# State-space constants moved to an earlier place and through DRAM, one rotation table for all batches, and gate weights loaded two jobs earlier, in a one-core decoder block

## The chip, the core and the metric

The kernel runs on one core of a Trainium2 chip. That core has five engines with an instruction stream each: TensorE (PE, the matrix multiplier, with its weight loads counted apart as PEld), VectorE (DVE), ScalarE (ACT), GpSimd (POOL) and SyncE (SP, which here issues nearly all DMAs). Each engine runs its stream in order and waits on semaphores for the others. The metric is the device time of one execution in microseconds (us), median over runs.

## What is computed

One decoder block over 16 meta tokens and 1024 positions of width 1024, in float32:

```python
h = layer_norm(concat(meta_tokens, x))
p = h @ w_in + b_in                     # columns: u_s5 | q | k | v | o | i | f | g_s5 | g_m
z = gelu(s5(u_s5)) @ s5_w_glu           # 32 groups of a complex diagonal recurrence
y_s5 = z[..., :D] * sigmoid(z[..., D:])
qk = silu(causal_conv(concat(q, k)))
hm = head_norm(mlstm(q, k, v, i, f))    # 4 heads, chunkwise
y_m = (sigmoid(o) * hm) @ m_w_out
mix = sigmoid(g_s5) * y_s5 + sigmoid(g_m) * y_m
h = layer_norm(alpha * h + mix @ w_o)
h = layer_norm(alpha * h + square(relu(h @ w_up + b_up)) @ w_down)
```

The S5 recurrence per group is x_t = Abar x_{t-1} + Bbar u_t with a complex diagonal Abar, and y_t = Re(C x_t) + D u_t. The kernel computes it in blocks of 8 positions: 130 blocks in a row, with matrices built from powers of Abar for what happens within a block, and a rotation table (the powers of Abar to the 8th, for 130 blocks) that turns the complex recurrence over blocks into a real scan.

## The kernel before

Float32 products are made of three passes: every operand is split into a high part (rounded to the matmul's format) and a low part (the rest), and `mm3` issues high x high, high x low and low x high (L226, L227, L228). A weight tile comes by DMA as `wraw`; ACT copies it to `whi` (L212) and DVE subtracts to get `wlo` (L213). This split is raised in priority, so that it stands early.

The program is a list of jobs. `ORDER` (L41) gives the first part: q0, q1, v0 and so on, where a q job makes q or k of one head (then the convolution), v the values and gates, o the output gate, u the S5 inputs, g an output gate's S5 half, m the matrices of the mLSTM output. Behind them come z0 to z7 (the GLU of the S5 output), then a stage `Seven` that computes the remaining gates and the mLSTM output product with seven products in place of eight (its left sides are sums and differences of blocks of h, its weights come pre-summed), then w_o and the feed-forward part.

Beside the jobs run *lanes*: generators that emit a few instructions at a time. `mm3` calls `pump(dt)` after every second term, which advances each lane by the time that the matmuls are reckoned to take; the numbers a lane yields (`C5`, `K5` and others, L44 to L55) are its pace. The lanes are ml (the mLSTM steps of the four heads), cv (convolution), s5c (S5 constants), s5 (S5 batches), s5g (GELU) and ah. A job `o` forces its head's mLSTM to be finished: it steps the lane until the head is ready. A scheduler then orders each engine's stream by its own reckoning of times; the order on each engine is fixed when the program is built.

Of an mLSTM step the document names: pk (L458), kw on ACT (L460), pS (L463), sw on DVE (L465), pn = C q (L473) and + v sw (L474), pu (L477), C updated on DVE (L482), the normaliser dd (L492 to L495), hraw on ACT (L496), the statistics (L497, L498). After four chunks come the head norm (ACT square root L172 with a table load, DVE L173 to L176, L506), eight transposes on PE (L513) and two copies on ACT (L514).

The S5 constants are made once for all (`s5_pre`, L579, started at job u0 by `S5_START`, L42) and then for each of four batches of eight groups when that batch's u tile is done (`s5_consts`, L674, added in L548): matrices `Mi` (input to state), `RS` (state to output), `Mx` (within a block) and the rotation table `T`, built by doubling: eight rounds of a complex product, six DVE operations each (L761 to L778). They stay in SBUF under `S5["m", b]`. `s5_batch` (L790) waits for them, then computes s5z on PE (L802), copies it by ACT and DVE (L812, L810), rotates it with T (L817 to L823), scans (L828), rotates back (L838 to L841), corrects (L846) and multiplies out on PE (L857, L858).

At z7 the pool `mid` is closed and a pool `ring` opened in its place; `begin()` loads eight blocks `rawb` of h (L991). After the last job, `first()` loads three tiles of gate weights into the ring (L1024), splits the first (L1042, L1043) and forms the differences of the h blocks (L1002), which become the left sides hT_hi (L997) and hT_lo (L998).

Of the kernel before, what the change touches and what calls it, by code (L numbers as in the profile page):

```python
# [9 lines left out]
F32 = mybir.dt.float32  # L10
# [4 lines left out]
P = 128  # L15
# [10 lines left out]
NB = LEN // 8  # L26
# [12 lines left out]
LN2_2 = math.log(2.0) - LN2_1  # L39
MAGIC = 1.5 * 2 ** 23  # L40
ORDER = "q0 q1 v0 q2 v1 q3 o1 o0 v2 o2 o3 u0 u1 v3 u2 g0 u3 g1 o4 o5 o7 o6 g2 g3 g5 g6 g4 g7 m0 m1"  # L41
S5_START = "u0"  # L42
NM = 2
SPLIT_UP = 200  # L44
PRE = 3
ZD = 1
ML = [2.4, 1.2, 1.68, 4.8]
NL = [0.88, 1.75, 1.75, 1.75]
C5 = [0.7, 0.98, 1.96, 0.49]
K5 = [1.7, 3.4, 1.7, 1.7]  # L50
Z5 = [1.0, 1.0, 1.0, 1.0]
D5 = [2.88, 1.22, 1.44, 1.44]
W5 = [2.21, 1.56, 2.6, 2.6]
# [59 lines left out]
def decoder_block(  # L113
# [80 lines left out]
    def load_w(job):  # L194
        job.raw = []
        for src, n in job.loads:
            r = slot("wraw") if ring[0] is None else ring[0].tile([P, 1024], F32, tag="wr", bufs=3, name="wraw")
            nc.sync.dma_start(r[:, :n], src)
            job.raw.append(r)

# [334 lines left out]
    def u_job(i):  # L535
        st = {}

        def evac(bi, c0, c1, ps):
            if bi == 0:
                st["u"] = slot("uT")  # L540
            o = st["u"][:, :LEN].rearrange("p (j c) -> p c j", j=8)
            a_.activation(o[:, c0 // 8:c1 // 8, :], ps.rearrange("p (c j) -> p c j", j=8), AF.Identity,
                          bias=bft[:, JU + i:JU + i + 1])

        def done():
            nc.sync.dma_start(us_dr[i * P:(i + 1) * P].rearrange("p j c -> p (j c)"), st["u"][:, :LEN])
            UD.add(i)
            lanes["s5c"].add(s5_consts(i))  # L548
            lanes["s5"].add(s5_batch(i))
        fm_job(JU + i, BLK, 0, evac, done)  # L550

# [118 lines left out]
        yield 1.3  # L670

    GEL = {}

    def s5_consts(b):  # L674
        E, ER = S5["E"], S5["ER"]
# [85 lines left out]
        T = slot("s5T")  # L761
        tc_, ts_ = (T[:, i * 520:(i + 1) * 520].rearrange("p (q c) -> p q c", q=4) for i in range(2))
        tmp = slot("s5tt")
        g_.memset(tc_[:, :, 0], 1.0)
        g_.memset(ts_[:, :, 0], 0.0)
        g_.tensor_copy(tc_[:, :, 1], S5["p8"][:, 0, q0:q0 + 4])
        g_.tensor_copy(ts_[:, :, 1], S5["p8"][:, 1, q0:q0 + 4])
        yield C5[b]
        n = 1
        while n < 129:  # L770
            m = min(n, 129 - n)
            sh = [P, 4, m]
            w1 = tmp[:, 0:4 * m].rearrange("p (q c) -> p q c", q=4)
            w2 = tmp[:, 512:512 + 4 * m].rearrange("p (q c) -> p q c", q=4)
            cmul(v_, tc_[:, :, n + 1:n + 1 + m], ts_[:, :, n + 1:n + 1 + m], tc_[:, :, 1:m + 1], ts_[:, :, 1:m + 1],
                 tc_[:, :, n:n + 1].to_broadcast(sh), ts_[:, :, n:n + 1].to_broadcast(sh), w1, w2)
            n *= 2
            yield C5[b]  # L778
        S5["m", b] = (RS, Mi, Mx, T)

    def u_load(b):
        U = slot("s5U")
# [221 lines left out]
    class Seven:  # L1004
# [8 lines left out]
        def load(self, i):  # L1013
            if i >= self.ntile():
                return
            r = ring[0].tile([P, 1024], F32, tag="wr", bufs=3, name="wraw")
            for j, (n, p) in enumerate(self.units[2 * i:2 * i + 2]):
                s = {5: 0, 6: 1, 7: 2, 3: 3}.get(n)
                if s is None:
                    t = self.w[self.i0 + 2 * p + (n == 4)].rearrange("p k f -> p (k f)")  # L1020
                    a = t[:, 0:512] if n == 1 else t[:, 512:1024]
                else:
                    a = ws_dr[self.p0 + p, s]
                tc.keep_in_program_order(nc.sync.dma_start(r[:, j * 512:j * 512 + 512], a))  # L1024
            self.raw[i] = r
# [117 lines left out]
    def gates_and_output():  # L1143
# [6 lines left out]
            for nm, kh, ch in (("12", 0, 1), ("22", 1, 1), ("11", 0, 0), ("21", 1, 0)):  # L1150
                R[nm] = raw_block(h_dr, kh, ch, META)

        def first():
            for i in range(3):
                g.load(i)
            g.split(0)
            sub(R["22"], R["12"], R["22"])
            sub(R["12"], R["12"], R["11"])
            sub(R["11"], R["11"], R["22"])
            to_home(R["11"], h01)  # L1160
            sub(R["21"], R["21"], R["11"])
            R.pop("11")
# [27 lines left out]
        return begin, first, run  # L1190

    def ln0_load(t):
        c0, n = rows0(t)
# [271 lines left out]
    jobs = all_jobs  # L1465
    ws = w_sums()
    next(ws)
    begin, first, run7 = gates_and_output()

    for i, j in enumerate(jobs):  # L1470
        if j.raw is None and j.w is None:
# [606 lines left out]
```

## Time and profile before

| what | before |
|---|---|
| median of 3 runs | 1565.78 us (1565.15 to 1569.24) |
| the profiled execution | 1566.04 us |
| its span in the trace | 1564.2 us |
| mean granted TensorE clock | 0.984 |
| DMA over the span | 261.32 MB, 137509 packets |

The span is what the profiler saw from the first to the last instruction; the rest of the profiled execution's time lies around it. The profile lists for each engine its busy time, a strip of 40 equal slices (39.1 us each) with tenths of busy time and of granted clock, groups of instructions by source line, and what ended the idle time before them. In the rows below, "out<-in" are the program's names for tiles.

### The profile page before, as it was taken

The numbers are of one execution on the slowest core, as the hardware profiler recorded it, in microseconds if no ns is written. First come the engines' busy times: TensorE is split into PE (matmuls) and PEld (weight loads), VectorE is DVE, ScalarE is ACT, GpSimd is POOL, SyncE is SP. The second block draws the span as 40 slices with busy tenths as digits, with TensorE's granted clock in tenths as the row PEclk, the third lists the DMA queues.
The fourth block names the chain that finished last, engine by engine and source line by source line (L and its number), as shares of the span: only waits on it lengthen the run. The fifth ranks groups of instructions, "written<-read, shape, count | busy, mean of one in ns | idle before, by whom it ended". The sixth has DMA issues, their size and how long they took to land.

```text
span 1564.2 us, 20543 instructions
## 1 busy us (share of the span) xinstructions
PE 1515.8 (97%) x7593; PEld 1278.7 (82%) x7593; DVE 1079.9 (69%) x2083; ACT 642.7 (41%) x982; POOL 102.2 (7%) x195
## 2 busy tenths in 40 slices
PE   8999999998999998989999999999999999999997
PEld 8998988996878886768788887888888888888886
DVE  7667555659867845677789675666666679766786
ACT  6523353333355433325534324444444534433340
POOL 0000001124031200000000001000000000000000
PEclk9999999998999999989999999999999999999999
DMA  8412324414354556775353328644443798667642
GB/s 311 159 57 61 100 62 129 122 37 112 104 129 103 164 182 218 279 269 195 108 170 114 108 76 247 225 158 149 147 149 123 248 363 322 230 229 236 216 166 108
DMA packets 137509, 261.32 MB, mean 167 GB/s; under 512 B 30768, under 2 KB 52984, under 8 KB 137352
## 3 DMA queue, kind: packets, MB, share of 16 engines
q1 hardware_dynamic: 111344, 233.00, 43.7%
q0 software_dynamic: 26064, 27.01, 7.1%
q8 instruction: 60, 0.98, 0.3%
q14 instruction: 41, 0.34, 0.1%
HBM read 188.78 MB, written 84.55 MB: 175 GB/s over the span
## 4 chain that ended last, share of the span: by engine, by line
PE 31%; issue 23%; DMA 3%; DVE 2%; ACT 0%; SPq 0%; POOL 0%; POOLq 0%; DVEq 0%
PE mm L228 7%; PE mm L227 7%; PE mm L226 7%; PE sd L227 3%; PE sd L226 3%; PE sd L228 3%; DMA wpre<-wu_dr 1%; DMA rawb<-h_dr 1%; DMA wu_dr<-wpre 1%; DMA wur<-in_wup_dram 0%; DVE wlo L1043 0%; DVE wlo L213 0%; DMA woraw<-in_wo_dram 0%; POOL wpre L1621 0%; SPq L991 0%
## 5 line engine op out<-in xcount | busy, mean ns | idle before, releaser
L226 PE MATMUL mm<-hT_hi,whi 128*128 128x512 f32 (+3 forms) x604 | 231.0, 382 | 8.0 <-ACT whi L1042 5.4
L228 PE MATMUL mm<-hT_hi,wlo 128*128 128x512 f32 (+3 forms) x604 | 226.7, 380 | 5.7 <-DVE wlo L213 3.7
L227 PE MATMUL mm<-hT_lo,whi 128*128 128x512 f32 (+3 forms) x604 | 229.1, 379 | 0.0
L226 PEld LDWEIGHTS mm<-hT_hi,whi 128*128 128x128 f32 x604 | 115.7, 192 | 26.6 <-ACT whi L1042 6.2
L228 PEld LDWEIGHTS mm<-hT_hi,wlo 128*128 128x128 f32 x604 | 115.0, 191 | 25.5 <-DVE wlo L213 4.3
L227 PEld LDWEIGHTS mm<-hT_lo,whi 128*128 128x128 f32 x604 | 115.6, 191 | 17.6 <-issue 0.4
L227 PE MATMUL sd<-dwl,dah 128*128 128x512 f32 x240 | 94.5, 394 | 0.0
L228 PE MATMUL sd<-dwh,dal 128*128 128x512 f32 x240 | 94.4, 394 | 0.0
L226 PE MATMUL sd<-dwh,dah 128*128 128x512 f32 x240 | 94.2, 393 | 0.0
L1773 ACT ACTIVATE dah<-da 128x1024 fp32r<-128x1024 f32 x56 | 58.7, 1052 | 86.2 <-PE sd L227 38.9
L1777 ACT ACTIVATE dwh<-wdr 128x1024 fp32r<-128x1024 f32 x56 | 58.9, 1053 | 84.0 <-DMA wdr<-in_wdn_dram 27.5
L1774 DVE TENSOR_TENSOR dal<-da,dah 128x1024 fp32r<-128x1024 f32 x56 | 68.2, 1219 | 23.8 <-ACT dah L1773 23.3
L228 PE MATMUL mm<-dwh,dal 128*128 128x512 f32 (+1 forms) x224 | 84.5, 378 | 0.0
L226 PE MATMUL mm<-dwh,dah 128*128 128x512 f32 (+1 forms) x224 | 84.4, 377 | 0.0
L227 PE MATMUL mm<-dwl,dah 128*128 128x512 f32 (+1 forms) x224 | 84.3, 377 | 0.0
L1778 DVE TENSOR_TENSOR dwl<-wdr,dwh 128x1024 fp32r<-128x1024 f32 x56 | 68.2, 1219 | 13.1 <-ACT dwh L1777 12.4
L226 PE MATMUL mm<-whi,hT_hi 128*128 128x256 f32 (+1 forms) x256 | 75.2, 294 | 0.0
L228 PE MATMUL mm<-whi,hT_lo 128*128 128x256 f32 (+1 forms) x256 | 74.7, 292 | 0.0
L227 PE MATMUL mm<-wlo,hT_hi 128*128 128x256 f32 (+1 forms) x256 | 73.8, 288 | 0.0
L213 DVE TENSOR_TENSOR wlo<-wraw,whi 128x1024 fp32r<-128x1024 f32 (+1 forms) x46 | 56.1, 1222 | 19.1 <-ACT whi L212 18.6
L228 PE MATMUL mm<-th,wul 128*128 128x512 f32 x156 | 61.6, 395 | 0.0
L227 PE MATMUL mm<-tl,wuh 128*128 128x512 f32 x156 | 61.5, 394 | 0.0
(474 smaller groups left out, 3703.1 us busy)
## 6 DMA issues: line engine op xcount, KB each, us to landing
da<-act_dr SPq DMA_DIRECT2D x56, 512.0 KB, 5.4
wdr<-in_wdn_dram SPq DMA_DIRECT2D x56, 512.0 KB, 6.3
wur<-in_wup_dram SPq DMA_DIRECT2D x32, 512.0 KB, 4.3
act_dr<-upy SPq DMA_DIRECT2D x64, 256.0 KB, 2.5
wraw<-in_wf_dram SPq DMA_DIRECT2D x30, 512.0 KB, 6.9
wu_dr<-wpre SPq DMA_DIRECT2D x21, 512.0 KB, 4.7
wpre<-wu_dr POOLq DMA_DIRECT2D x21, 512.0 KB, 5.0
act_dr<-upx SPq DMA_DIRECT2D x32, 256.0 KB, 2.8
```

The source lines that it names most:

```text
L213: todo.append(lambda e=v_, r=r, hi=hi, lo=lo, n=n: e.tensor_tensor(lo[:, :n], r[:, :n], f32(hi[:, :n]), op=OP.subtract))
L226: t_.matmul(ps, ah, bh, start=(i == 0 and part[0]), stop=False, skip_group_check=skip)
L227: t_.matmul(ps, ah, bl, start=False, stop=False, skip_group_check=skip)
L228: t_.matmul(ps, al, bh, start=False, stop=(i == n - 1 and part[1]), skip_group_check=skip)
L1773: a_.activation(ah[:, :D], a[:, :D], AF.Copy)
L1774: v_.tensor_tensor(alo[:, :D], a[:, :D], f32(ah[:, :D]), op=OP.subtract)
L1777: a_.activation(wh, raw[i], AF.Copy)
L1778: v_.tensor_tensor(wl, raw[i], f32(wh), op=OP.subtract)
```

## The change

`S5_START` becomes v0, the third job. There `s5_pre`, a new `s5_tables` and `s5_consts(0)` are queued in the lane s5c, and each `s5_consts(b)` queues the next. `s5_tables` builds one table for all 16 columns of constants in place of four (the products are four times as wide) and writes it to DRAM in four DMAs of 2048 pieces of 65 floats. `s5_consts` writes RS, Mi and Mx to DRAM, and `s5_batch` loads Mi, T, RS and Mx back. The pace numbers C5 and K5 of the lane change. The pool `mid` is closed and `ring` opened at z4 in place of z7, the first three tiles of gate weights are loaded at z6, ahead of the h blocks of z7, and the ring has four buffers in place of three.

```diff
-S5_START = "u0"
+S5_START = "v0"
...
-C5 = [0.7, 0.98, 1.96, 0.49]
-K5 = [1.7, 3.4, 1.7, 1.7]
+C5 = [1.9, 1.9, 1.9, 1.9]
+K5 = [1.7, 1.7, 1.7, 1.7]
...
-            r = slot("wraw") if ring[0] is None else ring[0].tile([P, 1024], F32, tag="wr", bufs=3, name="wraw")
+            r = slot("wraw")
...
             UD.add(i)
-            lanes["s5c"].add(s5_consts(i))
             lanes["s5"].add(s5_batch(i))
...
+    cs_dr = dram.tile([4, 3, P, 1024], F32, name="cs_dr")
+    ct_dr = dram.tile([2, P, 16, NB], F32, name="ct_dr")
+
+    def s5_tables():
+        lo, hi, tmp = ([slot("s5T"), slot("s5T")] for _ in range(3))
+        c1, s1 = (t[:, :1040].rearrange("p (q c) -> p q c", q=16) for t in lo)
+        c2, s2 = (t[:, :1040].rearrange("p (q c) -> p q c", q=16) for t in hi)
...
+        n = 1
+        while n < 64:
+            product(c1[:, :, n + 1:2 * n + 1], s1[:, :, n + 1:2 * n + 1], n, n, c1[:, :, 1:n + 1], s1[:, :, 1:n + 1],
+                    c1[:, :, n:n + 1], s1[:, :, n:n + 1])
+            n *= 2
+            yield 1.9
+        product(c2[:, :, 0:64], s2[:, :, 0:64], 64, 64, c1[:, :, 1:65], s1[:, :, 1:65], c1[:, :, 64:65], s1[:, :, 64:65])
+        yield 3.8
+        product(c2[:, :, 64:65], s2[:, :, 64:65], 128, 1, c1[:, :, 1:2], s1[:, :, 1:2], c2[:, :, 63:64], s2[:, :, 63:64])
+        for r in range(2):
+            nc.sync.dma_start(ct_dr[r, :, :, 0:65], (c1, s1)[r])
+            nc.sync.dma_start(ct_dr[r, :, :, 65:130], (c2, s2)[r])
...
-        S5["m", b] = (RS, Mi, Mx, T)
+        for i, t in enumerate((RS, Mi, Mx)):
+            nc.sync.dma_start(cs_dr[b, i], t[:, :1024])
+        CS.add(b)
+        if b < 3:
+            lanes["s5c"].add(s5_consts(b + 1))
...
-        while ("m", b) not in S5:
-            yield 0.5
-        RS, Mi, Mx, T = S5.pop(("m", b))
+        while b not in CS:
+            lanes["s5c"].step()
+        Mi, T, RS, Mx = (slot(n) for n in ("s5Mi", "s5T", "s5RS", "s5Mx"))
+        nc.sync.dma_start(Mi[:, :1024], cs_dr[b, 1])
...
-            r = ring[0].tile([P, 1024], F32, tag="wr", bufs=3, name="wraw")
+            r = ring[0].tile([P, 1024], F32, tag="wr", bufs=4, name="wraw")
...
-        def first():
+        def early():
             for i in range(3):
                 g.load(i)
+
+        def first():
             g.split(0)
...
         if j.tag == S5_START:
             lanes["s5c"].add(s5_pre())
+            lanes["s5c"].add(s5_tables())
+            lanes["s5c"].add(s5_consts(0))
...
-        if j.tag == "z7":
+        if j.tag == "z4":
             mid_ctx.close()
             ring_ctx = ExitStack()
             ring[0] = ring_ctx.enter_context(tc.tile_pool(name="ring", bufs=1, side="left"))
+        if j.tag == "z6":
+            early()
+        if j.tag == "z7":
             begin()
```

Line numbers in the rows of the change are its own: behind the new code they are 21 to 30 higher (L1024 becomes L1045, L991 becomes L1012, L817 becomes L838), while those of the mLSTM stay.

**PE, second half of head 0 and the start of v2.** Before, the head's last L474 (row 900) stands among matmuls of v2 (L226 to L228, `mm<-whi,hT_hi`), and its transposes follow 55 of them later, the last three of which are shown:

```order
953 L226 MATMUL mm<-whi,hT_hi 128x256
954 L227 MATMUL mm<-wlo,hT_hi 128x256
955 L228 MATMUL mm<-whi,hT_lo 128x256
956 L513 MATMUL pt<-ident,hraw 128x128 x2
957 L458 MATMUL pk<-ident,kT 16x128
958 L513 MATMUL pt<-ident,hraw 128x128 x2
959 L226 MATMUL mm<-whi,hT_hi 128x256
960 L513 MATMUL pt<-ident,hraw 128x128 x2
961 L227 MATMUL mm<-wlo,hT_hi 128x256
```

Now the step and the transposes follow each other, with S5 transposes (`s5p`) among them, ahead of v2's first matmuls (L340):

```order
909 L473 MATMUL pn<-C,qi 128x257
910 L474 MATMUL pn<-v_883,sw 128x257
911 L513 MATMUL pt<-ident,hraw 128x128 x2
912 L763 MATMUL s5p<-ident,s5P 128x128 x4
913 L513 MATMUL pt<-ident,hraw 128x128 x6
914 L763 MATMUL s5p<-ident,s5P 128x128 x4
915 L340 MATMUL mm<-whi,meta_hl 48x256 x8
```

The first half of the same head ends likewise; before, its two groups of four L513 stood among matmuls of o jobs. Now, ahead of the o0 job:

```order
849 L473 MATMUL pn<-C,qi 128x257
850 L474 MATMUL pn<-v_883,sw 128x257
851 L477 MATMUL pu<-v_883,kw 128x257
852 L513 MATMUL pt<-ident,hraw 128x128 x8
853 L458 MATMUL pk<-ident,kT 128x128
854 L463 MATMUL pS<-qT,kT 128x128
855 L473 MATMUL pn<-C,qi 128x257
856 L474 MATMUL pn<-v_883,sw 128x257
857 L477 MATMUL pu<-v_883,kw 128x257
858 L463 MATMUL pS<-qT,kT 128x128
859 L226 MATMUL mm<-hT_hi,whi 128x512
```

So the steps of the head have moved together, out of the matmuls of other jobs.

**DVE, end of the first half of head 3.** Before, the mLSTM rows (C, dd, sw, hst) stand here by themselves:

```order
794 L495 RECIPROCAL dd<-dd 128x1
795 L482 SCALAR_TENSOR_TENSOR C<-C,dec,pu 128x257
796 L497 BN_STATS hst<-hraw 128x6
797 L465 TENSOR_TENSOR sw<-pS,gB 128x128
798 L498 BN_AGGR hmv<-hst 128x2
```

Now S5 batch 3's rotation, scan and rotation back stand among them:

```order
719 L843 TENSOR_TENSOR s5Z<-s5w 128x520
720 L844 TENSOR_TENSOR s5Z<-s5w 128x520
721 L492 TENSOR_SCALAR dd<-pn 128x1
722 L849 SCALAR_TENSOR_TENSOR s5w<-s_r_993,s5Z 128x130 x4
723 L482 SCALAR_TENSOR_TENSOR C<-C,dec,pu 128x257
724 L849 SCALAR_TENSOR_TENSOR s5w<-s_r_993,s5Z 128x130
725 L493 SCALAR_TENSOR_TENSOR dd<-pn,ecol,dd 128x1
726 L849 SCALAR_TENSOR_TENSOR s5w<-s_r_993,s5Z 128x130 x3
727 L465 TENSOR_TENSOR sw<-pS,gB 128x128
728 L859 TENSOR_TENSOR s5Z<-s5w,s5T 128x512
729 L862 TENSOR_TENSOR s5w<-s5w,s5T 128x512
730 L495 RECIPROCAL dd<-dd 128x1
```

What moved is batch 3's work, which stood behind this half of the head before.

**SP, between the last z jobs and the gate stage.** Before (L1414 are the last writes of pre-summed feed-forward weights, L991 the h blocks, L1024 the gate weights):

```order
137 L198 DMA wraw<-in_wglu_dram 128x1024
138 L1414 DMA wu_dr<-wpre 128x1024 x7
139 L991 DMA rawb<-h_dr 128x2x512 x8
140 L1024 DMA wraw<-in_wf_dram 128x512 x6
141 L1024 DMA wraw<-ws_dr 128x512 x6
```

Now:

```order
167 L198 DMA wraw<-in_wglu_dram 128x1024
168 L1437 DMA wu_dr<-wpre 128x1024 x6
169 L1045 DMA wraw<-in_wf_dram 128x512 x6
170 L1437 DMA wu_dr<-wpre 128x1024
171 L1012 DMA rawb<-h_dr 128x2x512 x8
```

The six loads of gate weights changed places with the eight loads of h blocks, and stay behind six of the seven writes.

More of the change, by code (lines that the diff above doesn't have):

```diff
@@ L672, in decoder_block, with product @@
     GEL = {}
+    CS = set()
+    cs_dr = dram.tile([4, 3, P, 1024], F32, name="cs_dr")
[4 more added lines that the diff above has]
+        c2, s2 = (t[:, :1040].rearrange("p (q c) -> p q c", q=16) for t in hi)
+        g_.memset(c1[:, :, 0], 1.0)
+        g_.memset(s1[:, :, 0], 0.0)
+        g_.tensor_copy(c1[:, :, 1], S5["p8"][:, 0])
+        g_.tensor_copy(s1[:, :, 1], S5["p8"][:, 1])
+        yield 1.9
+        def product(oc, os, n, m, ac, as_, bc, bs):
+            w1, w2 = (t[:, 0:16 * m].rearrange("p (q c) -> p q c", q=16) for t in tmp)
+            sh = [P, 16, m]
+            cmul(v_, oc, os, ac, as_, bc.to_broadcast(sh), bs.to_broadcast(sh), w1, w2)
+        n = 1
[3 more added lines that the diff above has]
+            n *= 2
+            yield 1.9
+        product(c2[:, :, 0:64], s2[:, :, 0:64], 64, 64, c1[:, :, 1:65], s1[:, :, 1:65], c1[:, :, 64:65], s1[:, :, 64:65])
[4 more added lines that the diff above has]
+            nc.sync.dma_start(ct_dr[r, :, :, 65:130], (c2, s2)[r])
+        yield 1.9
     def s5_consts(b):
@@ L760, in s5_consts @@
         yield K5[b]
[L761 to L778, printed above, removed]
-        S5["m", b] = (RS, Mi, Mx, T)
+        for i, t in enumerate((RS, Mi, Mx)):
[3 more added lines that the diff above has]
+            lanes["s5c"].add(s5_consts(b + 1))
     def u_load(b):
@@ L793, in s5_batch @@
             yield 9.0
-        while ("m", b) not in S5:
-            yield 0.5
-        RS, Mi, Mx, T = S5.pop(("m", b))
+        while b not in CS:
+            lanes["s5c"].step()
+        Mi, T, RS, Mx = (slot(n) for n in ("s5Mi", "s5T", "s5RS", "s5Mx"))
+        nc.sync.dma_start(Mi[:, :1024], cs_dr[b, 1])
+        nc.sync.dma_start(T[:, :1040].rearrange("p (r q c) -> p r (q c)", r=2, q=4),
+                          ct_dr[:, :, 4 * b:4 * b + 4, :].rearrange("r p q c -> p r (q c)"))
+        nc.sync.dma_start(RS[:, :1024], cs_dr[b, 0])
+        nc.sync.dma_start(Mx[:, :1024], cs_dr[b, 2])
         uv = U[:, :8 * NB].rearrange("p (g c) -> p g c", g=8)
@@ L1189, in run @@
             y.run(lambda c, p: sdps() if c == "b" and p else mmps(), ym_evac, yhooks)
-        return begin, first, run
+        return early, begin, first, run
     def ln0_load(t):
@@ L1467, in decoder_block @@
     next(ws)
-    begin, first, run7 = gates_and_output()
+    early, begin, first, run7 = gates_and_output()
     for i, j in enumerate(jobs):
```

## The prediction, made before the changed kernel ran

> **What bounds the kernel now.** First the page's totals, then its clock line.
>
> ```profile
> PE 1515.8 (97%) x7593; PEld 1278.7 (82%) x7593; DVE 1079.9 (69%) x2083; ACT 642.7 (41%) x982; POOL 102.2 (7%) x195
> PEclk9999999998999999989999999999999999999999
> ```
>
> TensorE (PE) is busy for 97% of the span, so any change that keeps its matmuls, as this one does, can win only what PE waits, plus what it runs at a reduced clock. The two slices with an 8 are the 10th and the 18th: 352 to 391 us and 665 to 704 us. Next, what PE waited for. I asked the waits view stretch by stretch (waiting instruction, releaser, total, times, longest).
>
> ```profile
> PE gps L421 <- ACT gts L418: 2.0, 1, 2.0
> PE pu L477 <- ACT kw L460: 1.5, 1, 1.5
> ...
> PE mm L228 <- DVE wlo L213: 3.7, 1, 3.7
> PE s5k L741 <- DVE s5Ri L719: 2.9, 1, 2.9
> PE mm L226 <- DVE v L354: 1.3, 1, 1.3
> PE mm L226 <- ACT whi L212: 1.1, 1, 1.1
> ...
> PE mm L227 <- DVE gell L878: 3.1, 1, 3.1
> PE s5y L858 <- DVE s5w L846: 1.2, 1, 1.2
> ```
>
> The first two lie in 120 to 160 us, the next four in 340 to 400, the last two in 500 to 620. Then the same stretches as windows (busy time of each engine, granted clock, DMA share, GB/s):
>
> ```profile
> 160.00:340.00 180.00, 180.00 (x1139) 165.79 (x1138) 102.18 (x311) 72.22 (x118) 23.91 (x55) 1.00 0.33 92
> 365.00:390.00 25.00, 17.31 (x89) 14.49 (x89) 23.99 (x80) 10.37 (x15) 16.21 (x17) 0.73 0.41 113
> 455.00:480.00 25.00, 22.11 (x101) 17.24 (x101) 16.86 (x58) 16.76 (x22) 6.70 (x11) 1.00 0.28 60
> 670.00:680.00 10.00, 10.00 (x45) 8.13 (x44) 8.63 (x13) 3.82 (x6) 0.00 (x0) 1.00 0.97 366
> 690.00:700.00 10.00, 3.44 (x7) 2.32 (x8) 10.00 (x11) 3.17 (x3) 0.00 (x0) 0.57 0.58 202
> ```
>
> From 160 to 340 us PE never waits, with DVE at 57%. From 365 to 390 us DVE is full (23.99 of 25) and PE idles 7.7 us. Around 695 us PE waits again.
>
> **What the change removes.** (1) The table. Four doublings, one per batch, become one for all; the pile that fills DVE at 365 to 390 us goes. PE wins 3.7 + 2.9 + 1.3 + 1.1 = 9.0 us. The window's clock is 0.73, and at a floor of one half that means 0.27/0.5 x 25 = 13.5 us at half speed; 7.7 of the window are idle, and if 6 to 7 of the slow ones are busy, they lose half of themselves, about 3.5. Sum 12.5. (2) S5 ends earlier, before the GLU jobs: the waits for gell (3.1) and s5w (1.2) go, 4.3. (3) Waits at L421 and L477 (2.0 + 1.5) are taken over by a new pile there: 3.5. **Out: 20.3 us.**
>
> **What it adds.** The order of the changed kernel shows the same matmuls on PE, but other neighbours. I add up DVE's rows between two points at which it is tied to PE, and compare that with the matmuls that PE has there. Durations of one instruction (mean ns behind the bar):
>
> ```profile
> L817 DVE TENSOR_TENSOR s5w<-s5Z,s5T 128x520 f32<-128x520 f32 x4 | 2.8, 699 | 0.1
> L846 DVE TENSOR_TENSOR s5w<-s5Z,s5w 64x512 f32<-64x512 f32 x16 | 10.9, 684 | 0.2
> L828 DVE TENSOR_TENSOR_SCAN s5w<-s_r,s5Z 128x130 f32<-128x130 f32 x32 | 10.8, 401 | 0.0
> L213 DVE TENSOR_TENSOR wlo<-wraw,whi 128x1024 fp32r<-128x1024 f32 x40 | 48.8, 1222 | 19.1 <-ACT whi L212 18.6 <-DMA ys_dr<-s5Y 0.3
> L299 DVE SCALAR_TENSOR_TENSOR cy<-cpre,convt,cy 128x1040 f32<-128x1040 f32 x24 | 31.0, 1293 | 0.2
> L572 DVE TENSOR_TENSOR s5tt<-s5T 128x256 f32<-128x256 f32 x4 | 1.7, 425 | 0.1
> L514 ACT ACTIVATE hmF<-pt,mngt 128x512 f32<-128x512 f32 x16 | 10.5, 686 | 7.1 <-PE pt L513 7.1
> L460 ACT ACTIVATE kw<-pk,gB 128x128 f32<-128x128 f32 x28 | 10.1, 361 | 30.4 <-PE pk L458 30.3
> ```
>
> - **A, q2 to v1.** Six table products at each width: by the rows for 256 (0.43), 520 (0.70) and 1024 elements (1.22) the widths 1024, 512 and 256 cost 7.2, 4.0 and 2.4 us (overlap taken off), the narrower ones 3. With three convolution steps (1.29 each) and one of the like, five S5 products of 512 (0.65) and the wlo split itself, DVE has 25.3 us from v0's last eviction to the first wlo of v1; PE has 21.7 us of q2 by then (45 matmuls of 512 columns take 10 us). PE waits 3.6 us there, 0.8 to 2.9 more for the second wlo and conv rows between; I take 5.5. The gate rows behind them (L392, L405, L421) come 2.5 late. 8.0.
> - **B, first half of head 0.** One whole mLSTM step now stands between eight transposes L513 and the o0 job, without a matmul of another job. Ahead of the first L513, DVE has three L299 (3.9) and the head norm. Then k's activation on ACT and its multiply on DVE (some 3.5 with a table load, by rows of like size) stand ahead of the step's reciprocal, after which ACT runs L496, two L514, L460 and the whi split (0.47 + 0.69 + 0.69 + 0.36 + 1.05 = 3.3), and only then may o0's first matmul go. About 12 us against 5 of PE: 7.0.
> - **C, second half of head 0 and start of v2.** Here the trace shows the chain itself:
>
> ```profile
> 215.18 0.60 PE L474 MATMUL pn<-v,sw 128*128 128x257 f32 x2
> 215.81 0.16 DVE L492 TENSOR_SCALAR dd<-pn 128x1 f32<-128x1 f32 x1
> 216.51 0.47 ACT L496 ACTIVATE hraw<-pn,dd 128x256 f32<-128x256 f32 x1 [2.59 <-DVE dd L495]
> 217.00 1.28 ACT L172 ACT_TABLE_LOAD   x1
> 218.30 0.30 ACT L172 ACTIVATE hny<-hmv,eps_t 128x4 f32<-128x4 f32 x1
> 219.23 0.16 DVE L176 SCALAR_TENSOR_TENSOR hny<-hnu,hny 128x4 f32<-128x4 f32 x1
> 219.43 1.38 DVE L506 TENSOR_SCALAR hraw<-hraw,hmv,hny 128x256 f32<-128x256 f32 x4
> 222.11 0.38 PE L513 MATMUL pt<-ident,hraw 128*128 128x128 f32 x2
> ```
>
>   From the end of L474 to that of the first L506 (0.41) it is 4.1 us, and PE fills 6.3 to L513 with 55 matmuls of v2. In the changed order L513 stands right behind L474, so all 4.1 are bare; then two whi splits and a wlo (1.05, 1.05, 1.22) stand behind it on ACT and DVE before v2 can start, half hidden: 1.6. 5.7.
> - **Head 1**, where S5's copies now stand before L514, L460 and whi on ACT: 2.0.
> - **D, S5 batches 0 and 2** (their DVE work between mLSTM steps): 3.5.
> - **E, first half of head 3.** Batch 3's DVE work now falls among three mLSTM steps that PE issues with nothing between: six products of 520 (3.9 us, overlapped), eight scans (2.7), four of 512 (2.5), four L846 (2.7), and between them the steps' own rows and the head norm, about 5. That is 17 us to the L506 that L513 needs, while PE has 5: 12 to 13 us of wait. Before, the same place cost 2.9 (the 25 - 22.11 of 455 to 480 us). 10.
> - Clock after B, C and E: between 0 (455 to 480 us has 1.00 despite 2.9 us of waits) and 6 (half speed for 4 us after each, as at 690 to 700 with 0.57); I take 2, nearer the first.
> - **Gate junction.** The rows of before, z7's last product being issued at 688.86:
>
> ```profile
> 669.35 7.23 SPq L1414 DMA_DIRECT2D wu_dr<-wpre  x7
> 676.63 6.08 SPq L991 DMA_DIRECT2D rawb<-h_dr  x8
> 682.75 6.99 SPq L1024 DMA_DIRECT2D wraw<-in_wf_dram  x6
> 685.41 3.96 DVE L1002 TENSOR_TENSOR rawb<-rawb 128x1024 f32<-128x1024 f32 x3 [5.75 <-DMA rawb<-h_dr]
> 691.13 1.06 ACT L997 ACTIVATE hT_hi<-rawb 128x1024 fp32r<-128x1024 f32 x1 [6.81 <-DVE rawb L1002]
> 693.54 1.06 ACT L1042 ACTIVATE whi<-wraw 128x1024 fp32r<-128x1024 f32 x1 [1.35 <-DMA wraw<-in_wf_dram]
> 694.65 0.79 PE L226 MATMUL mm<-hT_hi,whi 128*128 128x512 f32 x1 [5.39 <-ACT whi L1042]
> 698.63 0.79 PE L228 MATMUL mm<-hT_hi,wlo 128*128 128x512 f32 x1 [1.91 <-DVE wlo L1043]
> ```
>
>   The waits name whi and wlo, which the early loads serve. But in SP's new order the six weight loads stand behind six of the last wu_dr writes (the first leaves at 669.35) and ahead of the rawb loads, while DMA is at 0.97 share: 1.5 MB at 366 GB/s holds rawb up by about 4 us. hT_hi then starts not at 691.1 but near 695.5, hT_lo (behind two more subtractions and a wlo) near 701. Loss 2.5; bounds -9 (both waits gone, 7.3, and the slow clock: 0.57 makes 8.6 us of half speed, of which PE is busy 3.4 and loses 1.7) and +5.
>
> **In: 8.0 + 7.0 + 5.7 + 2.0 + 3.5 + 10 + 2 + 2.5 = 40.7.** Net 40.7 - 20.3 = 20.4 us more. The profiled run took 1566.04 (span 1564.2, 1.8 around it); the median is 0.3 below. 1565.8 + 20.4 = **1586**.
>
> The constants' trips through DRAM (12 writes and 16 loads of about half a megabyte) lie in 100 to 500 us, where DMA has 0.28 to 0.41 share: nothing, at most 4 us if a weight load queues behind ct_dr's pieces of 260 bytes. The Trainium skill, "DMA: Bandwidth & Descriptors", section "Specifications", asks for at least 512 bytes for line rate, which speaks against those pieces; no run so far has such a store from these tiles, and by it the 4 would be likelier than the nothing. The 365 to 390 us window fell to 0.73 with no single wait above 3.7. The Trainium skill, "TensorE: Matmul & The Clock Gate", section "HAM oscillation — how this bites in real kernels", gives as its rule that only idle gaps above some 3.4 us bring the clock down; by it the clock term would be some 4, from C and E alone, and the time 1588. The trace speaks partly against it: 2.9 and 1.1 together had done it before the 3.7 came.
>
> **Rivals.**
> - Cheap bunches (faster). Place: B, C, head 1 and E. If the helpers run far enough ahead that these bunches cost nothing beyond what head 3 costs now, their 24.7 and the clock's 2 go: 1586 - 27 = 1559. They decide: below 1.9 us in all the kernel is faster by over 0.3% (4.7 us, about what a measurement tells from no change). For it: 160 to 340 us has no wait and DVE at 57%. Against: C's chain starts at PE's own L474, so nothing can run ahead. 0.10.
> - Each bunch costs the 2.9 us that the one bunch of the trace costs: 3 x 2.9 more, so 1559 + 9 = 1568. 0.14.
> - The loads pay at the gates, as the change says: the lower bound of the junction, 1586 - 2.5 - 9 = 1574. Against: the DMA share. 0.14.
> - DRAM trips hurt: loads of T, RS, Mx and the raw weights queue on SP, four batches x 3 us: 1598. 0.12.
> - The forecast: 0.50.
>
> **How the numbers follow.** Slower: forecast, paying loads and DRAM trips, and a little of the second rival: 0.78. Same: the rest of the second, 0.12. Faster: 0.10. The range from 1564 to 1602 takes in all but the first rival and the far end of the sum (E 13, clock 6, junction 5).
>
> **What would show it.** PE idle near 100 us before L344 (5 or more); before L513 and L226 at the ends of both halves of head 0 and the first of head 3, with S5 rows full on DVE; no stall between 340 and 400 us and clock 1.00 there; in the gate stage the first wait named for hT_hi or rawb, not whi. Waits below 10 us in heads 0 and 3 together, or a first gate matmul within 4 us of z7's last, would make it wrong.

## The result, and the profile after

| | before | changed |
|---|---|---|
| median, four runs each | 1566.03 us (1565.15 to 1569.24) | 1590.26 us (1587.66 to 1593.93) |
| ratio, 95% interval | | 1.0153 [1.0128, 1.0178] |
| span of the profiled execution | 1564.2 us | 1585.9 us |

The changed kernel is 24.2 us slower; the forecast was 1586. The page's totals and clock line of the changed kernel:

```profile
PE 1521.4 (96%) x7593; PEld 1282.3 (81%) x7593; DVE 1059.3 (67%) x1939; ACT 642.0 (40%) x982; POOL 93.5 (6%) x183
PEclk9998999999998999999999999999999999999999
```

DVE has 20.6 us less to do (1079.9 before), and the two old clock dips of the strip are gone; its two 8s now are the 4th and the 13th slice (39.6 us each), 119 to 159 us and 476 to 515 us. Where the time went is seen in windows of 100 us (start:end, length, busy time and count of PE, weight loads, DVE, ACT, POOL, granted clock, DMA share, GB/s). First before, then changed:

```profile
0.00:100.00 100.00, 93.00 (x740) 91.46 (x741) 73.17 (x147) 49.88 (x78) 6.26 (x21) 0.97 0.55 191
100.00:200.00 100.00, 96.55 (x610) 90.98 (x609) 59.36 (x183) 40.17 (x59) 7.57 (x15) 0.97 0.28 78
200.00:300.00 100.00, 100.00 (x611) 90.54 (x610) 55.08 (x184) 42.31 (x66) 10.37 (x19) 1.00 0.36 108
300.00:400.00 100.00, 90.64 (x590) 84.00 (x589) 79.15 (x257) 35.83 (x71) 32.13 (x61) 0.93 0.31 81
400.00:500.00 100.00, 97.11 (x477) 79.20 (x476) 68.50 (x203) 49.20 (x81) 18.13 (x30) 1.00 0.45 114
500.00:600.00 100.00, 95.68 (x462) 78.50 (x460) 64.13 (x131) 37.69 (x52) 13.30 (x26) 1.00 0.60 185
600.00:700.00 100.00, 87.64 (x351) 68.05 (x350) 63.45 (x85) 30.80 (x47) 2.08 (x2) 0.93 0.73 253
700.00:800.00 100.00, 99.94 (x427) 80.32 (x426) 71.66 (x76) 51.20 (x59) 0.00 (x0) 0.99 0.41 140
```

```profile
0.00:100.00 100.00, 90.26 (x715) 87.93 (x716) 78.32 (x252) 51.60 (x81) 9.14 (x33) 0.97 0.56 197
100.00:200.00 100.00, 93.19 (x616) 88.02 (x615) 81.75 (x173) 37.68 (x64) 18.70 (x40) 0.95 0.52 107
200.00:300.00 100.00, 91.04 (x532) 78.33 (x531) 62.80 (x174) 47.19 (x78) 24.68 (x52) 0.97 0.40 118
300.00:400.00 100.00, 98.90 (x658) 93.44 (x656) 53.03 (x159) 36.64 (x68) 10.09 (x20) 1.00 0.52 160
400.00:500.00 100.00, 83.90 (x421) 69.14 (x421) 59.58 (x134) 37.57 (x61) 4.20 (x4) 0.96 0.52 147
500.00:600.00 100.00, 94.11 (x411) 76.59 (x412) 33.03 (x60) 39.36 (x48) 11.45 (x9) 0.93 0.51 145
600.00:700.00 100.00, 95.99 (x404) 76.31 (x403) 53.54 (x71) 28.57 (x44) 2.87 (x3) 0.98 0.65 221
700.00:800.00 100.00, 97.04 (x406) 77.64 (x405) 77.22 (x82) 48.86 (x59) 0.00 (x0) 0.97 0.60 210
```

PE's idle time up to 800 us is what is missing to 100 in each row: 39.4 us before, 55.6 now, 16.1 more. What the reduced clock takes is, to first order, busy time times (1 - clock): 19.2 us before, 24.9 now, 5.7 more. (PE's busy time in the totals grew by 5.6 us with the same 7593 matmuls, which agrees.) Idle time and clock together are 21.8 us, against 21.7 by the spans, so everything that changed lies ahead of 800 us. By rows, idle and clock together: 300 to 400 us won 14.6 (the table's pile); 400 to 600 lost 24.7; 200 to 300 lost 11.7; 100 to 200 lost 5.1; 0 to 100 lost 2.7; 600 to 800 won 7.7. (The stages lie up to 38 us later in the changed kernel, so the borders are rough.) PE's waits in it, by the waits view (total, times, longest), from 100 us on; the stretches stand in order of time, within a stretch the longest wait first:

```profile
PE mm L344 <- DVE wlo L213: 3.6, 2, 3.4
...
PE pt L513 <- DVE hraw L506: 4.2, 1, 4.2
PE pt L513 <- DVE C L482: 1.7, 1, 1.7
...
PE pS L463 <- ACT hmF L514: 2.0, 1, 2.0
...
PE s5z L823 <- DMA s5yc<-ys_dr: 4.3, 1, 4.3
...
PE pu L477 <- DVE sw L465: 3.0, 2, 2.5
PE pt L513 <- DVE hraw L506: 3.0, 1, 3.0
PE pk L458 <- ACT hraw L496: 1.1, 1, 1.1
...
PE mm L226 <- ACT whi L212: 3.7, 1, 3.7
...
PE mm L228 <- DVE wlo L1064: 2.9, 1, 2.9
```

The first is place A of the prediction (128.9 us), the next two are C (235.0) and B (212.9), the fourth head 1 (292.4), the three in the middle E (488 to 502). Two were not in the sum: s5z at 434.6 us and whi at 562.3 us. The s5z row's releaser is misleading. SP and PE around it:

```profile
423.14 0.32 SPq L546 DMA_DIRECT2D us_dr<-uT  x1
423.55 0.38 SPq L813 DMA_DIRECT2D s5Mi<-cs_dr  x1
...
434.60 1.76 PE L823 MATMUL s5z<-s5U,s5Mi 128*128 128x130 f32 x8 [4.32 <-DMA s5yc<-ys_dr]
...
s5Mi<-cs_dr SPq DMA_DIRECT2D x1, 512.0 KB, 10.7
```

s5z multiplies by Mi. Mi's reload was issued at 423.55, behind the store of the u tile (L546), and took 10.7 us to land (last row, from the list of DMAs): 434.25, just ahead of the product. So the trip through DRAM stands on PE's path, because the reload is issued right ahead of its use. Batch 3's went the same way: its Mi took 8.3 us and landed just ahead of s5z at 474.38, for which PE waited 1.7 us.

### The profile page after: what moved, and what is told of

It reads as the page before. It is cut to its first block, busy times and chain, and to the rows that moved or that the text cites. A ratio compares the mean times of both kernels' runs of the same rounds, so it can differ in the third digit from the quotient of the medians.

```text
span 1585.9 us, 20447 instructions
## 1 busy us (share of the span) xinstructions
PE 1521.4 (96%) x7593; PEld 1282.3 (81%) x7593; DVE 1059.3 (67%) x1939; ACT 642.0 (40%) x982; POOL 93.5 (6%) x183
## 4 chain that ended last, share of the span: by engine, by line
PE 39%; issue 15%; DMA 1%; DVE 0%; SPq 0%; ACT 0%; POOLq 0%
PE mm L228 9%; PE mm L227 9%; PE mm L226 9%; PE sd L226 3%; PE sd L227 3%; PE sd L228 3%; DMA rawb<-h_dr 1%; PE ln L1593 0%; DMA wraw<-in_wf_dram 0%; DVE wlo L1064 0%; DVE rawb L1023 0%; SPq L1045 0%; POOLq L2102 0%; ACT whi L1063 0%; ACT hT_hi L1018 0%
## 5 line engine op out<-in xcount | busy, mean ns | idle before, releaser
L226 PE MATMUL mm<-hT_hi,whi 128*128 128x512 f32 (+3 forms) x604 | 228.1, 378 | 3.7 <-ACT whi L212 3.7
L228 PE MATMUL mm<-hT_hi,wlo 128*128 128x512 f32 (+3 forms) x604 | 226.9, 380 | 4.1 <-DVE wlo L1064 2.9
L228 PEld LDWEIGHTS mm<-hT_hi,wlo 128*128 128x128 f32 x604 | 115.1, 191 | 24.7 <-DVE wlo L1064 3.8
L226 PEld LDWEIGHTS mm<-hT_hi,whi 128*128 128x128 f32 x604 | 115.0, 190 | 21.9 <-ACT whi L212 4.2
L228 PE MATMUL sd<-dwh,dal 128*128 128x512 f32 x240 | 94.2, 393 | 0.0
L226 PE MATMUL sd<-dwh,dah 128*128 128x512 f32 x240 | 94.1, 393 | 0.0
L226 PE MATMUL mm<-dwh,dah 128*128 128x512 f32 (+1 forms) x224 | 84.5, 378 | 0.0
L228 PE MATMUL mm<-dwh,dal 128*128 128x512 f32 (+1 forms) x224 | 84.5, 378 | 0.0
L226 PE MATMUL mm<-whi,hT_hi 128*128 128x256 f32 (+1 forms) x256 | 75.6, 295 | 0.9 <-DVE mlo L348 0.9
L228 PE MATMUL mm<-whi,hT_lo 128*128 128x256 f32 (+1 forms) x256 | 74.5, 291 | 0.0
L228 PE MATMUL mm<-th,wul 128*128 128x512 f32 x156 | 61.6, 395 | 0.0
```

Source lines behind the costliest of these rows:

```text
L226: t_.matmul(ps, ah, bh, start=(i == 0 and part[0]), stop=False, skip_group_check=skip)
L228: t_.matmul(ps, al, bh, start=False, stop=(i == n - 1 and part[1]), skip_group_check=skip)
```

## The experiments

Each ratio is against runs of the kernel before on the same chip (medians of before 1564.5 to 1566.3 us).

**The two parts apart.** The first run has the gate part alone (ring at z4, weights at z6, four buffers), the second all but that.

> Only the gate part of the change: the ring opens at z4, the three weight tiles load at z6, four ring buffers; the S5 constants stay as before. The PE order up to the gates is that of before. My prediction's step (h blocks held up behind the weights): first gate matmul later than before, kernel 2 to 3 us slower, about 1568. Rival, from the trace of the changed kernel (the first gate matmul follows z7's last at once, one wait of 2.9 us for wlo remains): waits of 7.3 become about 3 and some slow clock goes, 4 to 6 us faster, about 1561.

> Only the S5 part of the change: constants from v0 on, one table, DRAM; gates as before. The PE order up to the gates is that of the changed kernel. If the two parts add: 1590 plus what the gates part wins, 1594 to 1596, and the two gate waits of 5.4 and 1.9 are back. If my prediction's junction step holds: 1587 to 1588.

Gates alone: 1561.74 us, ratio 0.9981 [0.9969, 0.9994], a gain of some 3 us. S5 alone: 1597.09 us, 1.0207 [1.0175, 1.0238]. So the loss is the S5 part's, and the gate loads win: 3 us in the kernel before, and 0.0054 of 1566, some 8, beside the S5 part (a rough figure, since the two intervals touch). Why they win shows in the changed kernel (SP, PE and DVE at the junction; z7's last product, then the gates' first):

```profile
702.89 4.15 SPq L1045 DMA_DIRECT2D wraw<-in_wf_dram  x6
707.68 6.70 SPq L1012 DMA_DIRECT2D rawb<-h_dr  x8
...
716.28 0.39 PE L228 MATMUL mm<-gelh,wlo 128*128 128x512 f32 x1
716.50 0.40 PE L226 MATMUL mm<-hT_hi,whi 128*128 128x512 f32 x1
...
717.67 2.58 DVE L1023 TENSOR_TENSOR rawb<-rawb 128x1024 f32<-128x1024 f32 x2 [1.00 <-DMA rawb<-h_dr]
```

The rawb loads are held up as foreseen, yet the first gate product starts without a gap, before DVE's row at 717.67 forms their differences: the first of the seven products takes a plain block of h, whose hT_hi had been made at the start of the kernel. Waits there: 2.9 us (before 5.39 + 1.91).

**Everything later.** `S5_START = "u0"`, as before, in the changed kernel.

> The changed kernel with the S5 constants started at job u0, as before; one table and the DRAM trips stay. In PE's order 4.0 and 6.4 us of other jobs' matmuls stand again between head 0's last steps and their transposes (0 and 0 in the changed kernel), and the table's 20 us of DVE leave the q2/v1 boundary. Theory (the early start piles DVE work and strips the cover): the waits at L344, L405 and head 0's L513 go, about 10 to 12 us with the clock, and a smaller pile comes back at u0: 1576 to 1583. Rival (DRAM trips and the SP queue cost the time): no gain from the place, 1588 to 1592, waits for s5z and whi around 435 and 560 us stay.

1631.19 us, 1.0418 [1.0388, 1.0448], outside both expectations. Up to 300 us all new waits were gone (only L421 and L477 as before), but now the constants are stored just before they are wanted (300 to 450 us, the longest waits):

```profile
PE s5z L823 <- issue: 10.5, 1, 10.5
PE s5p L763 <- DVE s5P L729: 7.3, 1, 7.3
PE s5y L878 <- DMA s5Mx<-cs_dr: 4.2, 1, 4.2
```

A write and a read of the same half megabyte then stand in PE's chain. This form of the change needs the early start.

**The reloads on another queue.** In the changed kernel `nc.sync.dma_start` of the four reloads becomes `g_.dma_start`.

> The changed kernel with the four reloads of each S5 batch issued from POOL's queue, not SP's. If the in-order SP queue is what held up s5z (4.3 us near 435) and one whi (3.7 us near 562): both go, 1581 to 1584. If the landing of the transfers themselves or the order of PE is the cause: 1588 to 1592.

1611.40 us, 1.0296 [1.0269, 1.0322]: worse than on SP and outside both expectations. GpSimd's issues for the first batch, and PE's waits before s5z:

```profile
332.28 1.95 POOL L995 DMA_DIRECT2D ws_dr<-in_wf_dram  x1 [0.16 <-issue]
333.43 1.40 POOL L813 DMA_DIRECT2D s5Mi<-cs_dr  x1
...
PE s5z L823 <- issue: 17.7, 2, 13.8
```

The first row is a weight sum, which adds 768 KB in DRAM; it took 30.8 us to land. Mi, issued behind it, took 31.1 and landed at 364.5, and s5z began at 364.61. In the changed kernel such a weight sum was under way as well (issued at 330.87, 33.6 us to land), and Mi's reload from SP took 4.1. So it was the place behind the weight sum on GpSimd's queue that held the reload up.

**The table alone, at two places.** The kernel before, with the gate part and one table (through `ct_dr`); RS, Mi and Mx as before, per batch and in SBUF.

```diff
-S5_START = "u0"
+S5_START = "v0"     # the second run: "v2"
...
-            while n < 129: ...            # the table of one batch in s5_consts
+        nc.sync.dma_start(T[:, :1040]..., ct_dr[:, :, 4 * b:4 * b + 4, :]...)
```

> Early gate loads and the one rotation table for all batches, computed from the first value tile on and kept in DRAM, as in the changed kernel; the other constants (RS, Mi, Mx) stay where the kernel before computes them, batch by batch, in SBUF, without a trip through DRAM. Theory (the table itself only costs its pile between q2 and v1; what bares heads 0, 1 and 3 is that the other constants come early, and their reload costs the waits at the start of S5): no wait of 2 us or more before L513 in head 0, none before s5z on a DMA; 1.5 to 3.6 us before L344; the four waits of 365 to 390 us mostly gone; 1564.5 - 3 (gate loads) - 12.5 (the pile) + 6 (q2 to v1) = 1552 to 1558. Rival (the early table is what costs, constants or not): the waits before L513 in head 0 are there as in the changed kernel, 1572 or more. Second rival (the pile at 365 to 390 us is made by the constants, not by the table): the four waits stay, 1564 to 1570.

> The same with the start moved from v0 to v2 (about 215 us), where the kernel before has no wait of PE until 340 us and DVE at 57%. Theory (a pile costs by where it falls, and there is room there): no wait of 2 us or more at L344 and none new in 160 to 340 us, four waits of 365 to 390 us mostly gone, 1564.5 - 3 - 12.5 = 1547 to 1553, faster than both kernels. Rival (the table's products, six at 1024 elements for the widest, pile up wherever they stand): 3 to 6 us of new waits between 215 and 340 us and some clock, 1553 to 1560. Second rival (the pile is the constants'): 1562 to 1567.

1572.16 us, 1.0039 [1.0026, 1.0051], and 1578.09 us, 1.0084 [1.0066, 1.0102]; so the theories missed by 14 us and by 25 (above their upper ends). The first time is the one that its first rival gave (1572 or more), but without the waits in head 0 by which that rival would come about. What they said of the old pile held in both, and of head 0 in the first: with the table at v0 there is no wait before L513 in head 0, and 300 to 400 us has

```profile
300.00:400.00 100.00, 98.83 (x674) 93.40 (x673) 72.53 (x183) 42.24 (x86) 24.71 (x51) 1.00 0.44 113
```

So the old pile was the table's, and head 0 is bared by the early constants, not by the table. But the gain of 14.5 us there is given back: 3.8 and 3.7 us of waits behind L344 (v L354, mlo L348), and in 400 to 600 us longer waits before s5y (3.4, before 1.2) and L513 (2.3, before 1.7) and a new one before s5k (2.1). With the table at v2, the rival's 5.6 us of waits at v2's whi and wlo came, and 5.9 before s5z on a DMA. There PE is busy for 93.76 of the first 100 us, against 90.25 with the start at v0 (93.00 and 90.26 in the kernels before and changed). But other runs with the start at v0 have 92.87 (the reloads one batch ahead, below) and 92.32 (S5 alone), so S5's early start beside the first layer norms explains that loss at most in part.

**The reloads one batch ahead.** In the changed kernel, batch b issues the four reloads of batch b + 1 ahead of its own s5y products.

```diff
+        if b + 1 < 4:
+            s5_reload(b + 1)
         (s5y products of batch b)
```

> The changed kernel, but each batch issues the four reloads of the next batch's constants before its own last products, so that batches 1 to 3 find them in SBUF; batch 0 and everything computed stay. Theory (the reloads stand in SP's order ahead of the raw weights and in front of s5z, and cost 4.3 + 1.7 us at s5z and 3.7 at whi L212): the waits before s5z go from the second batch on, and what was batch 0's 4.3 us stays or halves; 1580 to 1586. Rival (these waits only take the place of others, DVE being the bound there): 1588 to 1592.

1576.54 us, 1.0069 [1.0054, 1.0085]: below the theory's range. Against the changed kernel that is 0.0084 of 1566, 13 us. Two of its windows:

```profile
400.00:500.00 100.00, 92.98 (x471) 78.66 (x472) 68.17 (x161) 48.34 (x76) 8.05 (x6) 0.97 0.53 153
500.00:600.00 100.00, 99.14 (x448) 80.55 (x447) 32.70 (x41) 32.34 (x40) 9.13 (x8) 1.00 0.60 176
```

Idle time of 400 to 600 us fell from 22.0 to 7.9 us, and the waits at s5z on Mi and at whi in 562 us went (1.5 us remain at s5z, for the u tile, and 2.5 at s5y). The waits of head 3 fell from 8.7 to 4.2 (2.4 before L513, 1.3 before L473, 0.5 before L463), with 2.9 in the kernel before. That part is not the loads alone, since the edit also changed the order that the program is built with. Batch 3's work on DVE, from the rotation to the correction, fills these two stretches, the first in this run, the second in the changed kernel:

```profile
471.00:483.50 12.50, 11.21 (x52) 9.09 (x52) 12.38 (x27) 1.21 (x3) 0.00 (x0) 1.00 0.55 160
484.00:497.40 13.40, 8.04 (x33) 5.34 (x31) 13.26 (x31) 1.21 (x3) 0.00 (x0) 0.96 0.23 74
```

DVE is full in both. Here PE has another job's matmuls for nearly all of that time; in the changed kernel it has, from 486.3 us on, three steps of head 3 with nothing between. So the 13 us are what the late reloads cost together with where batch 3's work came to stand; the run does not tell the two apart.

**Room for head 0.** Three runs on top of that one spread the constants over more of PE's work, so that matmuls of another job stand again between head 0's last L474 and its transposes; the first with C5 = 4, the second with the table's steps spread as well, the third with C5 = 4 for batches 0 and 1 and 1.5 for 2 and 3.

> The changed kernel with the reloads issued one batch ahead, as in the run before, and one number more: a pause of 4 us of PE work instead of 1.9 between two steps of the constants (C5). The table and all else stay. By the order, PE then has 6.3 and 7.4 us of another job's matmuls in front of the transposes of the two halves of head 0, where the changed kernel has none (4.0 and 6.4 before). Theory (the waits of 1.7 and 4.2 us before L513 in head 0 and the 2.0 of head 1, with the slow clock behind them, come from the constants taking the places of the other job's matmuls): these go, 8 us of idle time and some 4 of clock, 1576.5 - 9 to 13 = 1563 to 1568; the 3.4 us at L344 stay. Rival (DVE is full there whatever the order, the waits only move to another place): 1573 to 1577.

> As the run before it, with the table's steps spread as well (5 us of PE work between two of them instead of 1.9, 10 instead of 3.8 after the widest). Theory (the 3.4 us before L344 are the pile of the six widest products and go when the steps are spread): 1556 to 1563, faster than the kernel before. Rival (DVE has the same work up to 215 us, and the wait moves to the gate rows behind L344 or to v1): 1563 to 1568, as the run before it.

> As the run of the slower constants, but with 4 us of PE work between two steps only for batches 0 and 1, and 1.5 for batches 2 and 3. By the order, heads 0 and 1 keep the matmuls of other jobs that they had in that run, and the last constants are stored before the reload that wants them. Theory (that run lost its gain of 200 to 300 us because batch 3's constants were still being computed and stored at 438 to 458 us, with their reload at 443 to 460 right behind and PE waiting 21.9 us for it): the waits of 21.9 and 7.7 us before s5z and s5y go, 200 to 300 us stays without waits of 3 us or more; 1576.5 (reloads ahead) - 11 (idle and clock of 200 to 300 us) + 3 (more waits between q2 and v1, as in that run) = 1566 to 1572. Rival (S5's batches collide with the heads at 400 to 500 us whenever head 0 is not held up): 7 us or more of waits before s5z stay, 1585 or more.

1600.71 us, 1.0228 [1.0211, 1.0246]; 1624.92, 1.0387 [1.0371, 1.0402]; 1607.00, 1.0270 [1.0249, 1.0292]. All three are above their theories and, but for the third, their rivals too; in the third its rival's sign came (7 us or more before s5z), though near 371 us. Head 0 went as foreseen in the first run: 200 to 300 us is busy for 97.77 us at clock 1.00, against 91.19 at 0.95 without the spreading, 11 us won. What was lost elsewhere is more, and the largest waits came through in-order queues. In the first, SP (of SP, ACT and PE):

```profile
460.35 0.32 SPq L816 DMA_DIRECT2D s5Mx<-cs_dr  x1
460.72 7.97 SPq L802 DMA_DIRECT2D s5U<-us_dr  x8
470.08 0.35 SPq L198 DMA_DIRECT2D wraw<-in_wf_dram  x1
...
485.00 1.06 ACT L212 ACTIVATE whi<-wraw 128x1024 fp32r<-128x1024 f32 x1 [22.83 <-DMA wraw<-in_wf_dram]
...
488.17 1.23 PE L831 MATMUL s5z<-s5U,s5Mi 128*128 128x130 f32 x4 [21.95 <-DVE sw L465]
```

Batch 3's constants were late. Their store waited for them on SP (Mx at 457.56), their reload and the u loads behind that, and behind those the next weights, which left SP at 470.08. PE waited 21.95 us, not for the constants but for whi and for what stood behind wlo on DVE. In the second run, head 0 lost 9.0 us at L463, and s5z waited 17.0 and 25.6; the 25.6 are the same chain, with the next weights leaving SP at 491.16. In the third no wait of that kind was left at batch 3, and another queue struck (POOL, ACT, PE):

```profile
364.40 4.54 POOL L788 DMA_DIRECT2D s5Mx<-s5Kt  x9 [28.77 <-DMA ws_dr<-in_wf_dram]
368.93 0.33 POOL L753 MEMSET s5Rr<- 128x256 f32 x1
...
369.29 1.05 ACT L757 ACTIVATE s5Rr<-s5bb 64x64 f32<-64x64 f32 x4 [21.30 <-POOL v L336]
...
370.89 1.45 PE L831 MATMUL s5z<-s5U,s5Mi 128*128 128x130 f32 x5 [18.71 <-ACT hraw L496]
```

The pieces of Mx stood behind a weight-sum transfer on GpSimd's queue, GpSimd behind the pieces, its memset of the next batch's Rr behind them, ACT's copies into Rr behind the memset, and the mLSTM's hraw behind the copies.

**That chain cut, and batch 0 alone spread.** The first run moves the memset; the second has it too, with C5 = [4, 1.9, 1.9, 1.9].

```diff
-        g_.memset(Rr[:, 576:832], 0.0)
+        v_.memset(Rr[:, 576:832], 0.0)
```

> As the run before it, with one instruction moved: the memset of Rr in the constants goes from GpSimd to VectorE. Theory (the 18.7 us before s5z were a chain through two engines: a weight-sum transfer of 768 KB on GpSimd's queue held up the pieces of Mx behind it, these held up GpSimd, whose memset of the next batch's Rr came 28.8 us late, ScalarE's copies into Rr waited for that, and head 2's and S5's evictions waited behind them on ScalarE): the 18.7 us go, and with them some 4 us of clock in 300 to 400 us; 1607 - 19 to 24 = 1583 to 1588. Rival (PE waits there for constants that come late whatever ScalarE does, since the same transfer holds up Mx itself): a wait of 10 us or more before s5z or s5y stays at 330 to 400 us; 1597 or more.

> The changed kernel with the reloads one batch ahead, the memset of Rr on VectorE, and 4 us between the steps of batch 0's constants alone (1.9 for the others), so that head 0 keeps its 6.3 and 6.9 us of another job's matmuls and all constants are stored long before their reload. Theory (head 0's waits and clock, 11 us, can be had back without a late constant): no wait of 3 us or more in 200 to 300 us and none of 5 in 300 to 500 us; 1576.5 - 11 + 3 (q2 to v1, as in the two runs with slower constants) = 1566 to 1571. Rival (each shift of the lanes moves the collision into another stage): a wait of 5 us or more appears between 300 and 560 us; 1576 or more.

1599.65 us, 1.0211 [1.0194, 1.0229]: ACT no longer waits for GpSimd there and the 18.7 us became 3.2, which shows the chain. But the run is only 7 us faster than the one before it, and slower than its theory: a wlo wait of 5.2 us appeared in the same stretch and s5y's wait grew from 5.7 to 7.8. The other: 1581.95 us, 1.0099 [1.0072, 1.0127], the rival's number though no single new wait reaches its 5 us: head 0's waits before L513 went, while 100 to 200 us lost 3.4 us of idle time more, 400 to 500 lost 2.6, and the clock fell in both.

No version with the S5 part beats the kernel before. The gate part alone does, by an amount (0.19%) below what the prediction's text took as measurable.

## Why the prediction was right, and which of its steps were not

The sign, the range and the outline of the mechanism (the gain of the pile is outweighed by new bunches at the heads) were right. That the sum came within 4 us of the time is luck: errors of some 20 us each way cancelled. B, D with E, and the junction were too high by some 5, 8 and 7 us; the trips through DRAM and the clock were too low by some 10 and 7, and 2.7 us in the first 100 were not foreseen. Of the signs that the text named, the waits in heads 0 and 3 together came to 14.6 us, above its 10, and there was no stall between 340 and 400 us. But a first gate matmul within 4 us of z7's last, which it named as a sign of being wrong, did come (716.28 and 716.50).

- **The pile's removal, 12.5.** Right: 14.6 by the row of 300 to 400 us, 14.5 with the table alone.
- **gell and s5w, 4.3; L421 and L477, 3.5.** The first went, but a whi wait of 3.7 stood in its place until the reloads were issued ahead. The second gave way to 2.1 at L405 and L458, which is counted with A.
- **A, 8.0.** 6.6 measured (3.6 at L344, mlo 0.9, L405 and L458): right.
- **B 7.0, C 5.7, head 1 2.0.** 1.7, 4.2 and 2.0. C and head 1 held; B was mis-sized: I put DVE's and ACT's rows of the bunch behind one another, and most of them had been done by the time that PE came to L513.
- **D 3.5 and E 10.** E's mechanism was right and its size too high: 8.7 in head 3, 5.8 more than before, with batch 3's work on a full DVE beside steps that have nothing between. With the reloads one batch ahead other matmuls cover most of that work, and 1.3 more than before is left. Of D there were some 2 us of short waits at 437 to 443 us.
- **DRAM trips, 0, at most 4.** This is the step that failed. I argued from the DMA share in 100 to 500 us (0.28 to 0.41; the row of 400 to 500 us has 0.45) and asked whether the transfers have room. The question was where they stand in SP's order and how long before their use: issued right ahead of s5z, they cost 4.3 and 1.7 us before it, and the 3.7 at whi went with them when they were issued a batch ahead. That run is 13 us faster in all, with the clock behind the waits and with the better place of batch 3's work. The rival "DRAM trips hurt" named SP's queue.
- **Gate junction, +2.5.** Wrong in sign. I took the first gate product to need an hT_hi made from rawb, and that was not so. The weights' wait went and nothing took its place for long: 7.3 us of waits became 2.9, and the part alone won some 3 us.
- **Clock, 2 added, 3.5 removed.** Mis-sized. In the rows it is 5.7 more in all: 6.3 went with the pile and 2.3 at the gates, and 14.4 came in 100 to 300 and 400 to 600 us. Gaps below 3 us in a row were enough, as at head 3:

```profile
492.00:496.00 4.00, 1.82 (x7) 1.11 (x7) 3.94 (x10) 0.84 (x2) 0.00 (x0) 1.00 0.00 0
496.00:500.00 4.00, 1.23 (x2) 0.50 (x2) 3.67 (x13) 1.95 (x3) 0.00 (x0) 0.55 0.00 0
```

  In finer windows the clock is 1.00 up to 496.2 us and 0.50 from 496.4 on. From 487.9 us until then PE had five gaps of 0.5 to 1.1 us, 3.3 together, and 1.1 us of a sixth, which became 2.5; the gap of 3.0 came later. The rule of the Trainium skill, "TensorE: Matmul & The Clock Gate", section "HAM oscillation — how this bites in real kernels", that idle gaps above some 3.4 us bring the clock down, does not cover this. Nor did the kernel before need 2.9 and 1.1 together at its pile, as I read it: the clock halved at 374.0 us, after the gap of 2.9 and before that of 1.1.

What stays open: with the reloads out of the way the changed kernel is still 11 us slower than before. The rows put this on the first 300 us (start, A, heads 0 and 1: idle and clock together 35.9 us there, 16.1 before), but each attempt to take head 0's part away moved waits to other stages, so it was not shown that the early constants could be had without it. Keeping them in SBUF from the start, without the trip, was not tried; they would hold 16 of the program's 30 large buffers, and whether these can be spared was not shown.

## What to carry to other kernels

What a tile's way to DRAM and back cost here was not its bytes but when its reload was issued and behind what: look up what stands ahead of the reload on the issuing engine, and issue it one stage before its use (13 us here, with the change of order that came along). When a stage is moved in a kernel with one in-order stream per engine, its DMA issues and its small helpers (a memset, a copy) move too, and a wait of any of them holds up everything behind it, however unlike. And a forecast that is right in total may be wrong in half of its terms; only runs with one part undone tell which.

## What the runs showed of the hardware that was not expected

- A transfer on GpSimd's queue can hold up that engine's own instructions: in the third spread run a weight-sum transfer that adds 768 KB in DRAM took 34.6 us to land, the pieces of Mx issued behind it (20 to 32 KB) up to 32.2 us, those issued after it had landed (4 to 20 KB) 1.6 to 1.7, and GpSimd stood still for 28.8 us. The Trainium skill, "DMA: Bandwidth & Descriptors", section "Anatomy of one DMA — SWDGE (gpsimd) path", gives a fit by which such a transfer would take an estimated 3.8 us; for this adding one the measurement is nine times that.
- Storing the table in pieces of 260 bytes was slow: in the changed kernel four stores of 520 KB took 16.7 us to land (median), SP was held for 13.8 us while issuing the last two, and the window

```profile
120.00:135.00 15.00, 10.46 (x55) 8.89 (x54) 14.93 (x30) 3.56 (x5) 0.00 (x0) 0.76 0.84 135
```

  shows 135 GB/s at a DMA share of 0.84, where 670 to 680 us before had 366 at 0.97. The Trainium skill, "DMA: Bandwidth & Descriptors", section "Specifications", asks for at least 512 bytes for line rate, and the trace agrees. It cost PE nothing that could be seen: the waits there are named for DVE, which was full.
- The half megabyte of Mi took 4.1 us to reload at 330 us and 10.7 us at 423 us. Three more reloads stood behind it both times; at 423 us a store of 520 KB had been issued right ahead of it, and loads of ys came behind. Which of these made the difference was not tested.
